# Later stores, states written in place and earlier small weights in a scheduled hybrid decoder layer

## The chip, the core and the metric

The kernel runs on one core of a Trainium2 chip. The metric is the device time of one execution in microseconds (us); the number given is the median of the runs. The engines in the profile are PE (TensorE, matrix products; PEld are its weight loads), DVE (VectorE), ACT (ScalarE), POOL (GpSimd) and SP (SyncE, whose queue issues the transfers).

## The reference

One layer of a hybrid decoder, for a prompt of 2048 tokens and for 8 samples of 8 new tokens (2112 tokens in all), width 1024. Cut to what matters:

```python
xn = rms_norm(x, norm_pre)
z = xn @ w_in                      # 1024 x 4096: v_pool, g_pool, u_lru, g_lru, 1024 columns each
# pool: mean over the last 2, 4, 8 or 16 tokens (4 groups of 256 columns) less the token; a
# 256 x 256 map by group; a scale. A sample's first means reach into its 15 state rows
y_pool = pool_map(window_mean(v_pool) - v_pool) * pool_scale
# lru: causal convolution of width 4, then gates from 128 x 128 blocks and a linear recurrence
xs = conv4(u_lru)
r, i = sigmoid(xs @ wa + ba), sigmoid(xs @ wx + bx)
a = exp(-8 * r * softplus(-lam))
h[t] = a[t] * h[t - 1] + xs[t] * i[t] * sqrt(1 - a[t] ** 2)
mixed = concat(y_pool * silu(g_pool), h * silu(g_lru))
out = x + rms_norm(mixed @ w_out, norm_post)
```

Outputs are the rows for prompt and samples and the new states (the last 15 pool rows, 3 convolution rows, last h).

## The kernel before

**Products.** Everything is float32. Each operand is split in a high part (a cast by ScalarE) and a low part (a subtraction, by VectorE or GpSimd, L310), and each product is three: high·high, high·low, low·high. `hi_lo` (L825) is this split for half tiles of the input weights.

**Tokens and quads.** The tokens lie along the columns, in three macro-tiles m = 0, 1, 2 of 704 columns (the last holds 640 prompt tokens and the 64 sample tokens). The 4096 columns of w_in are 16 quads for each macro-tile: four groups p of the kinds V (pool in), G (pool gate), U (lru in) and L (lru gate). m = 0 uses plain products, with raw weights from w_in split on the way. m = 1 and 2 use a seven-product (Winograd) form of each quad: `a1V`, `e2G` and so on are its partial results. It needs seven sums of quarters of the normalised tokens (X11, T1, T2, X22, X21, T3, T4) and seven of the weights. The weight sums are made and split while m = 0 runs, stored to DRAM (`wsd`), and loaded six products ahead by `w_step` (L870). For the late quads (all of U and L of m = 1, and V and G of its first group) the sums are made in m = 1 itself. The half tiles of weights form a ring of seven.

**The chains around the products.** The partial results are copied or added (L980, L976) into tiles: `e` for V, `u` for U, `g` for the gates. From `e`, `pool_chain` (L1043) makes window sums, `dh` and `dl`, and `pool_map` (L1107) the map with the weights `pw`, into `g`, stored to `mixed` (L1129). From `u`, `conv_chain` (L1134) makes `xs` (L1157, VectorE), its high part `xh` (L1162, ScalarE) and its low part `xl` (L1164, GpSimd); `gate_mm` (L1169) multiplies them by the weights `lw` to the gates `r` and `i`; `lru_chain` (L1192) runs the recurrence, and GpSimd multiplies by the gate and SP stores it to `mixed` (L1233 to L1243). The tiles `t` (16 in all) and `e` (6) are pools: a quad begins when enough are free. The small weights `pw` and `lw` are loaded for m = 0 by `load_small` (L897: L907, L910), split (L915) and stored for the later macro-tiles (L920). For m = 2, `quad_begin` (L930) puts the samples' 15 state rows into `e`: SP loads them into a tile `sp`, of which there is one buffer (L944), and GpSimd copies them into place (L945).

**Between macro-tiles**, `x_chain` (L1251) normalises the next tokens into XA, and `transition` (L1304) makes the seven sums from XA and splits them into XN as their products come up: T2 and T4 in two spare tiles (`t2_tiles`, once `dg` and `rt`), the others in XA.

**The out-projection**, from about 843 us on, is again seven products per block of tokens (p1 to p7); `a` tiles come back from `mixed` (L426), weights from w_out or from combinations of it in DRAM, `wtd` (made and stored in L1365 to L1380, loaded in L378 and split in L1392).

**The order.** A planner in the kernel file writes the order of every engine. The products stand in a fixed row of slots (L1411). The chains are generators that ask for engine time, and a job is granted to the engine that can start it earliest by the planner's own clocks. "t" moves a job's ready time, "D" lets it issue a transfer once that time lies within the present slot. Every engine and the SP queue execute in program order, so an instruction that waits holds back all behind it. For a transfer this reads:

```python
elif e == "t":
    job["ready"] += arg
elif e == "D" and job["ready"] <= end:
    pass
```

Transfers all go through the one SP queue.

Of the kernel before, what the change touches and what calls it, by code (L numbers as in the profile page):

```python
# [10 lines left out]
F32 = mybir.dt.float32  # L11
# [48 lines left out]
TABLE_COST = 1.3  # L60
X_LEAD = (6, 5)
# [6 lines left out]
def hymba_kernel(  # L68
# [827 lines left out]

    def load_small(m, kind, p):  # L897
# [7 lines left out]
        r = t_tile(f"{kind}r{p}")[:, :512]  # L905
        if kind == "pw":
            nc.sync.dma_start(out=r, in_=pool_w[p])  # L907
        else:
            for j in range(2):
                nc.sync.dma_start(out=r[:, 256 * j:256 * (j + 1)], in_=lru_w[2 * p + j])  # L910

        def work():
            yield "t", 4.0
            yield "A", 0.62
            AC.copy(out=t[:, 0, :], in_=r)  # L915
            yield "V", 0.75
            tsub(t[:, 1, :], r, t[:, 0, :].bitcast(F32))
            t_done(1)
            yield "D", 0
# [10 lines left out]
    def quad_begin(q):  # L930
# [3 lines left out]
        for j, blk in enumerate(blocks(kind, p)):  # L934
            if kind == "V":
# [6 lines left out]
                if m == LM:  # L942
                    sp = sb.tile([P, N_S, PB], F32, tag="sp", bufs=1, name=f"sp{blk}")
                    nc.sync.dma_start(out=sp, in_=st_pool[blk])  # L944
                    G.tensor_copy(out=seq8(E, PB + PW, SP_ST, 0, PB), in_=sp)  # L945
# [10 lines left out]
            else:  # L956
                dst.append(t_tile(f"g{blk}_{m}"))

# [84 lines left out]
    def pool_chain(q):  # L1043
# [3 lines left out]
        c = L * 0.00125 + 0.08  # L1047
        ds = []
        for j, blk in enumerate(blocks("V", p)):
# [19 lines left out]
            yield "V", 1.05  # L1069
# [17 lines left out]
        if not m:  # L1087
# [19 lines left out]
    def pool_map(q, j, c):  # L1107
# [12 lines left out]
        def evac():  # L1120
            V.scalar_tensor_tensor(out=g[:, cs], in0=Y, scalar=col(C_SCALE, blk), in1=g[:, cs],  # L1121
                                   op0=ALU.mult, op1=ALU.mult)
            if c == 1:
# [3 lines left out]
                def store():  # L1127
                    yield "D", 0
# [5 lines left out]
    def conv_chain(q, j):  # L1134
# [4 lines left out]
        yield "?", lambda: (not prev or prev.get("gates")) and t_free() >= (3 if j or m else 4)  # L1139
# [15 lines left out]
        for k in range(CB):  # L1155
            yield "V", 1.2
# [6 lines left out]
        yield "G", 1.95  # L1163
        tsub(xl, xs, xh.bitcast(F32), G)  # L1164
# [27 lines left out]
    def lru_chain(q, j, r, gi, v):  # L1192
# [4 lines left out]
        yield "V", 0.95  # L1197
# [6 lines left out]
        yield "V", 0.95  # L1204
        u = t_chain(f"w{m}_{b}")[:, :n]
        V.scalar_tensor_tensor(out=u, in0=r, scalar=1.0, in1=v, op0=ALU.add, op1=ALU.mult)
        yield "V", 0.95
# [4 lines left out]
        yield "V", 0.95  # L1212
# [3 lines left out]
        yield "V", 1.1  # L1216
# [3 lines left out]
        yield "V", 1.8  # L1220
# [8 lines left out]
        yield "G", 2.2  # L1229
        sg = Q[lq]["dst"][j]  # L1230
        if m < LM:
            G.tensor_copy(out=hh[:, b:b + 1], in_=r[:, MW - 1:MW])
            G.tensor_tensor(out=sg[:, :MW], in0=sg[:, :MW], in1=r, op=ALU.mult)  # L1233
        else:
# [3 lines left out]
            G.tensor_tensor(out=sg[:, :PW], in0=sg[:, :PW], in1=r[:, :PW], op=ALU.mult)  # L1238
            G.tensor_tensor(out=as8(sg[:, PW:MW]), in0=as8(sg[:, PW:MW]), in1=seq8(r, PW, SC_ST, CB, S_S),
                            op=ALU.mult)  # L1240
        t_done(1)
        yield "D", 0
# [8 lines left out]
    def x_chain(m):  # L1251
# [34 lines left out]
        for k in range(KT):  # L1286
            yield "V", 0.95
            a = stage_x(k // HK)[:, k % HK, :]
            V.scalar_tensor_tensor(out=a, in0=a, scalar=col(C_NP, k), in1=rt[:, :MW], op0=ALU.mult, op1=ALU.mult)
        t2_tiles[:] = [dg, rt]  # L1290
# [3 lines left out]
    t2_tiles = []  # L1294
# [9 lines left out]
    def transition(m):  # L1304
# [4 lines left out]
        src = {"X11": X(0, 0), "T1": X(0, 0), "T2": t2_tiles, "X22": X(1, 1), "T3": X(0, 1), "X21": X(1, 0),  # L1309
               "T4": t2_tiles}  # L1310
        done = set()

        def put(n, eng="V"):
# [6 lines left out]
            if n == "T4":  # L1320
                t_done(2)

        def chain():
# [36 lines left out]
    def combos_chain():  # L1360
# [9 lines left out]
        for k in range(KT):  # L1370
            yield "D", 0
            r, nxt = nxt, load(k + 1) if k + 1 < KT else None
            for j, o, a, b in ((T1, (0, 0), (0, 1), (0, 0)), (T3, (0, 1), (1, 1), (0, 1)),
# [4 lines left out]
                def store(j=j, k=k, o=r[o]):  # L1378
                    yield "D", 0
# [4 lines left out]
    def region_chain(r, j, k0, k1):  # L1384
# [3 lines left out]
        for k in range(k0, k1):  # L1388
# [4 lines left out]
            yield "V", 0.75  # L1393
# [484 lines left out]
```

## Time and profile before

| what | before |
|---|---|
| median of 3 runs (lowest to highest) | 1195.79 us (1193.86 to 1197.48) |
| the profiled execution | 1194.03 us, span 1192.3 us |
| mean granted clock of PE | 0.98 |
| PE busy, and idle in the span | 1132.6 us, 59.7 us |
| DVE, ACT, POOL busy | 902.9, 653.8, 253.3 us |
| transfers | 322.10 MB, mean 270 GB/s |

Rows of the profile name an instruction as line, engine, operation, written tile, read tiles. In square brackets, or after the last bar of a group, stands how long the engine was idle before it and what released it. The clock column is the mean clock granted to PE in that stretch, as a share of full speed. The view of waits lists per engine the waiting operation, what released it, the total, how often, and the longest. SPq rows are transfers being issued.

### The profile page before, as it was taken

The page shows a single profiled execution, that of the slowest core. Times are in us where ns is not written, and L with a number is a line of the kernel's source. Part 1 is how long each engine was busy: PE and PEld are TensorE (multiplying, and loading weights), DVE is VectorE, ACT ScalarE, POOL GpSimd, SP SyncE. Part 2 cuts the span into 40 slices and gives each one's busy share as a digit, 9 for nine tenths or more (in the row PEclk, how much of TensorE's full clock was granted, in tenths as well). Part 3 has the DMA queues.
Part 4 walks back from the last instruction along what each step waited for, and adds up shares of the span by engine and source line. Part 5 has one row for each costly group of instructions (what it writes and reads, how often), then busy time and mean ns, then how long its engine had stood idle before and what let it go on. Part 6 is the DMA issues. An engine that isn't in the chain of part 4 may idle for free. (4 is left out here: it accounts for less than half of the span.)

```text
span 1192.3 us, 17811 instructions
## 1 busy us (share of the span) xinstructions
PE 1132.6 (95%) x6274; PEld 1055.3 (89%) x6274; DVE 902.9 (76%) x1356; ACT 653.8 (55%) x1109; POOL 253.3 (21%) x284
## 2 busy tenths in 40 slices
PE   7999998988999999999799989999989999999996
PEld 6999998988899999988799979999868888888885
DVE  6779783897978858677688958767586668778777
ACT  5455747758665748666557736455844233344222
POOL 4201100200523030200443512214020003211232
PEclk9999998998999999999899989999989999999998
DMA  9278696936799898998699989999669776776553
GB/s 336 116 269 328 223 330 235 356 139 235 276 315 318 291 333 309 385 360 294 221 334 371 351 340 393 342 333 324 186 169 277 206 212 197 210 233 199 159 177 123
DMA packets 173368, 322.10 MB, mean 270 GB/s; under 512 B 17568, under 2 KB 79264, under 8 KB 173280
## 3 DMA queue, kind: packets, MB, share of 16 engines
q1 hardware_dynamic: 173280, 320.97, 77.9%
q8 instruction: 49, 0.80, 0.3%
q14 instruction: 39, 0.32, 0.1%
HBM read 218.51 MB, written 102.15 MB: 269 GB/s over the span
## 5 line engine op out<-in xcount | busy, mean ns | idle before, releaser
L438 POOL TENSOR_TENSOR xr<-ac,xr 128x512 f32<-128x512 f32 x27 | 46.6, 1745 | 225.8 <-DVE ac L578 120.1
L1157 DVE SCALAR_TENSOR_TENSOR xs<-u,parT,xs 128x704 f32<-128x704 f32 (+1 forms) x72 | 85.3, 1193 | 12.0 <-ACT xs L1146 11.6
L445 PE MATMUL p<-XN,s 128*128 128x512 f32 (+1 forms) x224 | 87.7, 392 | 3.9 <-ACT s L132 3.9
L446 PE MATMUL p<-XN,s 128*128 128x512 f32 (+1 forms) x224 | 87.5, 391 | 0.0
L447 PE MATMUL p<-XN,s 128*128 128x512 f32 (+1 forms) x224 | 87.3, 390 | 0.0
L310 POOL TENSOR_TENSOR xl<-xs,xh 128x704 fp32r<-128x704 f32 (+1 forms) x24 | 45.9, 1910 | 144.1 <-ACT xh L1162 93.9
L241 PE MATMUL zL<-XN,wL 128*128 128x352 f32 x384 | 64.5, 328 | 0.7 <-DVE wL L310 0.7
L241 PEld LDWEIGHTS zL<-XN,wL 128*128 128x128 f32 x384 | 63.2, 192 | 1.3 <-DVE wL L310 1.3
L558 ACT ACTIVATE p<-ac 128x512 f32<-128x512 f32 (+1 forms) x32 | 18.8, 587 | 74.2 <-DVE ac L438 74.2
L241 PE MATMUL y<-dh,pw 128*128 128x352 f32 x192 | 55.2, 329 | 4.4 <-ACT pw L915 2.4
L132 ACT CAST s<-a 128x512 fp32r<-128x512 f32 x48 | 28.8, 616 | 52.8 <-DVE a L438 39.2
L445 PEld LDWEIGHTS p<-XN,s 128*128 128x128 f32 x224 | 42.6, 190 | 14.1 <-ACT s L132 4.4
L438 DVE TENSOR_TENSOR a<-a,a 128x512 f32<-128x512 f32 x48 | 32.9, 690 | 28.5 <-DMA a<-mixed 24.7
L445 PE MATMUL p<-XN,a 128*128 128x512 f32 x137 | 54.0, 394 | 0.0
L447 PE MATMUL p<-XN,a 128*128 128x512 f32 x137 | 54.0, 394 | 0.0
L446 PE MATMUL p<-XN,a 128*128 128x512 f32 x137 | 54.0, 394 | 0.0
L1121 DVE SCALAR_TENSOR_TENSOR g<-y,parT,g 128x352 f32<-128x352 f32 x48 | 27.9, 580 | 31.1 <-PE y L241 31.0
L446 PEld LDWEIGHTS p<-XN,s 128*128 128x128 f32 x224 | 42.6, 190 | 9.8
L447 PEld LDWEIGHTS p<-XN,s 128*128 128x128 f32 x224 | 42.4, 189 | 10.0 <-DVE s L135 0.2
L241 PE MATMUL zU<-XN,wU 128*128 128x352 f32 x288 | 50.3, 329 | 0.0
L241 PE MATMUL zV<-XN,wV 128*128 128x352 f32 x288 | 48.1, 323 | 0.3 <-ACT wV L827 0.2
L241 PEld LDWEIGHTS zU<-XN,wU 128*128 128x128 f32 x288 | 48.1, 194 | 0.0
(352 smaller groups left out, 3293.3 us busy)
## 6 DMA issues: line engine op xcount, KB each, us to landing
a<-mixed SPq DMA_DIRECT2D x112, 256.0 KB, 4.0
mixed<-g SPq DMA_DIRECT2D x48, 352.0 KB, 5.6
w2V<-wsd SPq DMA_DIRECT2D x28, 512.0 KB, 6.9
w2G<-wsd SPq DMA_DIRECT2D x28, 512.0 KB, 5.6
w2U<-wsd SPq DMA_DIRECT2D x28, 512.0 KB, 6.7
w2L<-wsd SPq DMA_DIRECT2D x28, 512.0 KB, 6.8
wsd<-XN SPq DMA_DIRECT2D x27, 512.0 KB, 4.6
w1V<-wsd SPq DMA_DIRECT2D x24, 512.0 KB, 5.3
```

The costliest lines, as they stand in the source:

```text
L132: hi_eng.copy(out=hi, in_=src)
L241: nc.tensor.matmul(out, lhsT=lhsT, rhs=rhs, start=start, stop=stop)
L310: (eng or V).tensor_tensor(out=out, in0=a, in1=b, op=ALU.subtract)
L438: (eng or nc.vector).tensor_tensor(out=out, in0=a, in1=b, op=op)
L445: nc.tensor.matmul(out, lhsT=ah, rhs=wh, start=start and k == 0, stop=False)
L446: nc.tensor.matmul(out, lhsT=ah, rhs=wl, start=False, stop=False)
L447: nc.tensor.matmul(out, lhsT=al, rhs=wh, start=False, stop=stop and k == KT - 1)
L558: nc.scalar.activation(out=junk, in_=o, func=AF.Square, accum_out=st[:, g:g + 1])
L1121: V.scalar_tensor_tensor(out=g[:, cs], in0=Y, scalar=col(C_SCALE, blk), in1=g[:, cs], op0=ALU.mult, op1=ALU.mult)
L1157: V.scalar_tensor_tensor(out=xs, in0=E[:, k:k + n], scalar=col(C_CW + 8 * k, b), in1=xs, op0=ALU.mult, op1=ALU.add)
```

## The change

Five things are done. (1) Stores are given to the queue some time after their data are ready: 4.0 us for weight sums and small weights, 2.0 for `mixed` and `wtd`. The "t" before "D" puts them later in the program's order. (2) The pool states are loaded straight into `e`, as 128 x 8 x 15 numbers with gaps between the rows; the tile `sp` and its copy are gone. (3) The small weights of groups 1 to 3 in m = 0 are loaded when the quad V or U begins, and not when their chain comes to them; this holds one more `t` tile meanwhile, and the conditions on free tiles are raised by one. A delay of 4.0 in front of their split is gone. (4) T2 and T4 are made in place, in the quarter X(0,0) of XA that T1 was made in: T2 as X22 less T1, once T1 is split. The low parts of X22 and X21 are on VectorE, their jobs start with the transition, and the two spare tiles are freed earlier. (5) The low part `xl` is on VectorE. Besides, the planner's durations are changed, and its clock of VectorE is moved on by 0.6 at each long GpSimd job. The core of the diff:

```diff
+LAG = 4.0
+MLAG = 2.0
+XL_ON = "V"
+SG_ON = "G"
...
     def grant(job, start):
         e, dur = job["req"][:2]
+        if e == "G" and dur > 1.5:
+            clock["V"] = max(clock["V"], T[0]) + 0.6
...
     def hi_lo(hi, lo, src, store=None):
...
-        yield "V", 0.75
+        yield "V", 0.71
         tsub(lo, src, hi.bitcast(F32))
         if store:
+            yield "t", LAG
             yield "D", 0
             nc.sync.dma_start(out=w_key(*store[1:]), in_=store[0].bitcast(F32))
...
+    def small_early(kind, p):
+        r = small_raw[kind, p] = t_tile(f"{kind}r{p}")[:, :512]
+        if kind == "pw":
+            nc.sync.dma_start(out=r, in_=pool_w[p])
+        else:
+            for j in range(2):
+                nc.sync.dma_start(out=r[:, 256 * j:256 * (j + 1)], in_=lru_w[2 * p + j])
...
         def work():
-            yield "t", 4.0
             yield "A", 0.62
             AC.copy(out=t[:, 0, :], in_=r)
...
             t_done(1)
+            yield "t", LAG
             yield "D", 0
...
                 if m == LM:
-                    sp = sb.tile([P, N_S, PB], F32, tag="sp", bufs=1, name=f"sp{blk}")
-                    nc.sync.dma_start(out=sp, in_=st_pool[blk])
-                    G.tensor_copy(out=seq8(E, PB + PW, SP_ST, 0, PB), in_=sp)
+                    nc.sync.dma_start(out=seq8(E, PB + PW, SP_ST, 0, PB), in_=st_pool[blk])
...
+        if m == 0 and p and kind in "VU":
+            small_early({"V": "pw", "U": "lw"}[kind], p)
...
                 def store():
+                    yield "t", MLAG
                     yield "D", 0
                     nc.sync.dma_start(out=mixed[:, blk, m * MW:(m + 1) * MW], in_=g[:, :MW])
...
         AC.copy(out=xh, in_=xs)
-        yield "G", 1.95
-        tsub(xl, xs, xh.bitcast(F32), G)
+        yield XL_ON, 0.9 if XL_ON == "V" else 1.95
+        tsub(xl, xs, xh.bitcast(F32), {"V": V, "G": G}[XL_ON])
...
         t_done(1)
+        yield "t", MLAG
         yield "D", 0
         nc.sync.dma_start(out=mixed[:, 8 + b, m * MW:(m + 1) * MW], in_=sg[:, :MW])
...
-        src = {"X11": X(0, 0), "T1": X(0, 0), "T2": t2_tiles, "X22": X(1, 1), "T3": X(0, 1), "X21": X(1, 0),
-               "T4": t2_tiles}
+        src = {"X11": X(0, 0), "T1": X(0, 0), "T2": X(0, 0), "X22": X(1, 1), "T3": X(0, 1), "X21": X(1, 0),
+               "T4": X(0, 0)}
...
+            yield "?", lambda: "T1" in done
             yield "V", 1.75
-            x_raw(t2_tiles, X(1, 1), X(0, 0))
+            x_raw(src["T2"], X(1, 1), src["T1"])
             x_jobs["T2"] = spawn(put("T2"), clock["V"] + HOP, rank=0)
-            x_jobs["X22"] = spawn(put("X22", "G"), T[0], rank=0)
...
             yield "?", lambda: "T2" in done
             yield "V", 1.75
-            x_raw(t2_tiles, X(1, 0), t2_tiles)
-            x_jobs["X21"] = spawn(put("X21", "G"), T[0], rank=0)
+            x_raw(src["T4"], X(1, 0), src["T2"])
...
+        for n in ("X22", "X21"):
+            x_jobs[n] = spawn(put(n), rank=0)
...
                 def store(j=j, k=k, o=r[o]):
+                    yield "t", 2.0
                     yield "D", 0
                     nc.sync.dma_start(out=wtd[:, j, k, :], in_=o)
...
-                while t_free() < {"V": 0}.get(q[2], 2) or (q[2] == "V" and (e_free() < 2 or not sums_done(*q[:2]))):
+                while t_free() < {"V": 0, "U": 2}.get(q[2], 2) + (m == 0 and q[2] in "VU") or (q[2] == "V" and (e_free() < 2 or not sums_done(*q[:2]))):
...
             for k in range(5, KT):
                 src = w_load("b11", k)
                 w_split(0, k, src)
+            clock["A"] += 4.4
+            clock["V"] += 5.0
```

Where the instructions stand now, at three places that the prediction speaks of (line numbers differ between the two files).

The SP queue before, near the end of the first macro-tile; `lwr` are the raw lru weights of the last group, `wr1U` raw weights of m = 1:

```order
L874 DMA w1G_1_3161<-wsd 128x1024
L832 DMA wsd<-w1V_7_3137 128x1024
L874 DMA w1V_4_3201<-wsd 128x1024
L910 DMA lwr_3206<-in_lru_w 128x256 x2
L832 DMA wsd<-w1G_5_3181 128x1024
L339 DMA wr1U_11_3256<-in_w_in 128x512
```

And now; `wr0L` are the raw weights of the last quad of m = 0:

```order
L839 DMA wsd<-wL_22_2557 128x1024
L839 DMA wsd<-wU_11_2656 128x1024
L912 DMA lwr_2730<-in_lru_w 128x256 x2
L343 DMA wr0L_11_2733<-in_w_in 128x512
L343 DMA wr0L_12_2735<-in_w_in 128x512
L343 DMA wr0L_21_2737<-in_w_in 128x512
```

The load of the last group's lru weights has moved from among the weights of m = 1 to ahead of the raw weights of the last quad of m = 0.

The SP queue before, at the start of the out-projection; `w` are weights for its products, `a` tiles of `mixed`, `g_2` the last gates of m = 2:

```order
L378 DMA w_3_8667<-wtd 128x512
L378 DMA w_4_8696<-wtd 128x512
L426 DMA a_0_0_8721<-mixed 128x4x128
L426 DMA a_0_0_8723<-mixed 128x4x128
L426 DMA a_0_1_8725<-mixed 128x4x128
L426 DMA a_0_1_8727<-mixed 128x4x128
L378 DMA w_5_8752<-wtd 128x512
L1243 DMA mixed<-g_2_8348 128x704
L378 DMA w_6_8780<-wtd 128x512
L378 DMA w_7_8791<-wtd 128x512
```

And now, up to the same two weights:

```order
L382 DMA w_4_8637<-wtd 128x512
L382 DMA w_5_8666<-wtd 128x512
L1771 DMA gp<-in_norm_post 128x1024
L1144 DMA mixed<-g_2_8178 128x704
L430 DMA a_0_0_8694<-mixed 128x4x128
L430 DMA a_0_0_8696<-mixed 128x4x128
L430 DMA a_0_1_8698<-mixed 128x4x128
L430 DMA a_0_1_8700<-mixed 128x4x128
L382 DMA w_6_8730<-wtd 128x512
L382 DMA w_7_8746<-wtd 128x512
```

The store of the lru gate is no longer between w_5 and w_6; it comes fourteen rows after w_7.

GpSimd before, where m = 1 passes into m = 2; `e_2` are the first two V tiles of m = 2, the last row the low parts of X22 and X21:

```order
L953 COPY u_1_5475<-hu 128x3
L941 COPY e_2_5768<-hp 128x15
L945 COPY e_2_5768<-sp_5770 128x8x15
L941 COPY e_2_5773<-hp 128x15
L945 COPY e_2_5773<-sp_5775 128x8x15
L310 TENSOR_TENSOR XN<-XA,XN 128x1408 x2
```

VectorE now, at the same place; XA rows are raw sums in place, XN rows low parts:

```order
L314 TENSOR_TENSOR XN<-XA,XN 128x1408
L990 TENSOR_TENSOR g_1_5555<-a1L_5556,g_1_5555 128x352
L314 TENSOR_TENSOR XN<-XA,XN 128x1408
L314 TENSOR_TENSOR dl_31_5707<-s_1_8_5552,dh_31_5671 128x704
L314 TENSOR_TENSOR XN<-XA,XN 128x1408
L314 TENSOR_TENSOR XA<-XA 128x2x352 x2
L1221 SCALAR_TENSOR_TENSOR w_4_5761<-rg_4_5355,xs_1_5044 128x704
L314 TENSOR_TENSOR XN<-XA,XN 128x1408
L1135 SCALAR_TENSOR_TENSOR g_1_5078<-y_5749,parT,g_1_5078 128x352
L314 TENSOR_TENSOR XA<-XA 128x2x352 x2
```

All seven low parts of this transition now stand in VectorE's row, four of them within these ten rows, and no copy of states stands on GpSimd ahead of them.

More of the change, by code (lines that the diff above doesn't have):

```diff
@@ L904, in load_small @@
             return
[L905 to L910, printed above, removed]
+        if (kind, p) not in small_raw:
+            small_early(kind, p)
+        r = small_raw.pop((kind, p))
         def work():
-            yield "t", 4.0
             yield "A", 0.62
             AC.copy(out=t[:, 0, :], in_=r)
-            yield "V", 0.75
+            yield "V", 0.71
             tsub(t[:, 1, :], r, t[:, 0, :].bitcast(F32))
             t_done(1)
+            yield "t", LAG
             yield "D", 0
@@ L1086, in pool_chain @@
         yield "?", lambda: not prev or prev.get("maps")
-        if not m:
+        if not m and not p:
             yield "?", lambda: t_free() >= 1
@@ L1138, in conv_chain @@
         prev = Q.get((m, p - 1, "U") if p else (m - 1, NG - 1, "U"))
-        yield "?", lambda: (not prev or prev.get("gates")) and t_free() >= (3 if j or m else 4)
+        yield "?", lambda: (not prev or prev.get("gates")) and t_free() >= (3 if j or m or p else 4)
         t_live[0] += 3
@@ L1232, in lru_chain @@
             G.tensor_copy(out=hh[:, b:b + 1], in_=r[:, MW - 1:MW])
-            G.tensor_tensor(out=sg[:, :MW], in0=sg[:, :MW], in1=r, op=ALU.mult)
+            SGE.tensor_tensor(out=sg[:, :MW], in0=sg[:, :MW], in1=r, op=ALU.mult)
         else:
@@ L1739, in p1_chain @@
                             prep_11(g + 2)
+                            clock["A"] += 1.3
+                            clock["V"] += 1.4
                         if g + 4 < 5:
```

35 lines of the change are left out of this document (17 added, 18 removed).

## The prediction

> **What bounds the kernel now.** I read the page's busy times first:
>
> ```profile
> PE 1132.6 (95%) x6274; PEld 1055.3 (89%) x6274; DVE 902.9 (76%) x1356; ACT 653.8 (55%) x1109; POOL 253.3 (21%) x284
> ```
>
> TensorE (PE) is busy for 95% of a span of 1192.3 us, and the change leaves its products alone. So the change can only win time in which TensorE stands still, and time in which it runs slowly. The view of waits of that engine names both the waiting operation and what came last for it (columns: total us, times, longest):
>
> ```profile
> PE a2V L239 <- DMA w2V<-wsd: 6.7, 2, 5.8
> ...
> PE e2V L239 <- POOL XN L310: 5.0, 1, 5.0
> PE r L241 <- ACT xh L1162: 4.4, 1, 4.4
> PE p L445 <- ACT s L132: 3.9, 1, 3.9
> PE y L241 <- ACT pw L915: 2.4, 1, 2.4
> PE a1U L239 <- DVE u L976: 2.2, 1, 2.2
> PE a2L L239 <- DMA w2L<-wsd: 1.7, 1, 1.7
> ...
> PE r L241 <- ACT lw L915: 1.5, 1, 1.5
> PE y L241 <- DVE pw L310: 1.5, 1, 1.5
> ...
> PE r L241 <- POOL u L951: 1.4, 1, 1.4
> PE p L241 <- ACT a L132: 1.3, 1, 1.3
> PE e2V L239 <- DVE XN L310: 1.2, 1, 1.2
> ...
> PE r L241 <- DVE lw L310: 0.9, 1, 0.9
> ...
> PE r L241 <- POOL xl L310: 0.8, 1, 0.8
> ```
>
> Few waits, nearly all single, each at its own place. (The 1.4 named after `u` is, by the operation it stands in front of, a product with `xl`.) Then I cut an 8 us stretch from the end of each larger wait, and looked at the granted clock:
>
> ```profile
> 185.50:193.50 8.00, 6.52 (x24) 6.06 (x25) 4.46 (x7) 8.00 (x16) 1.86 (x5) 0.57 0.62 222
> 270.27:278.27 8.00, 6.62 (x23) 6.38 (x24) 5.27 (x7) 6.10 (x10) 1.75 (x3) 0.57 0.91 327
> 324.79:332.79 8.00, 7.07 (x25) 6.78 (x26) 7.27 (x12) 5.99 (x9) 0.00 (x0) 0.57 1.00 352
> 584.62:592.62 8.00, 7.98 (x37) 7.69 (x38) 2.61 (x5) 2.20 (x3) 3.22 (x2) 0.76 0.77 263
> 706.89:714.89 8.00, 8.00 (x37) 8.00 (x38) 4.10 (x7) 0.45 (x1) 0.00 (x0) 0.72 1.03 415
> 879.27:887.27 8.00, 8.00 (x22) 6.27 (x23) 6.92 (x12) 3.23 (x7) 1.87 (x3) 0.61 0.75 205
> ```
>
> Columns are the stretch, its length, busy us of PE, its weight loads, VectorE (DVE), ScalarE (ACT) and GpSimd (POOL), the clock, DMA share and GB/s. After six waits the clock is 0.57 to 0.76, where a stretch without them has 1.00 (below). A wait therefore costs itself and, behind it, (1 − clock) × the busy time of PE: 2.8, 2.8, 3.0, 1.9, 2.2 and 3.1 us in the order of the rows.
>
> After the wait of 2.2 for `u` there is no such loss:
>
> ```profile
> 555.50:563.50 8.00, 7.98 (x49) 7.80 (x50) 4.13 (x6) 5.49 (x8) 0.00 (x0) 1.00 0.91 321
> ```
>
> **Part by part.** All in the profiled run's time, 1194.03 us. It lies 1.8 below the median of the runs before, so 1.8 is added at the end.
>
> *Small weights a quad or more earlier.* The first part of this (A) is the pool map at 185, the second (C) the lru gates at 324:
>
> ```profile
> 176.65 0.44 SPq L907 DMA_DIRECT2D pwr<-in_pool_w  x1
> ```
>
> ```profile
> 184.83 0.62 ACT L915 CAST pw<-pwr 128x512 fp32r<-128x512 f32 x1 [10.46 <-DMA pwr<-in_pool_w]
> ```
>
> ```profile
> 324.12 0.62 ACT L915 CAST lw<-lwr 128x512 fp32r<-128x512 f32 x1 [0.91 <-DMA lwr<-in_lru_w]
> ```
>
> The load goes out 8.2 us ahead of the cast; ScalarE waits 10.46 for it, the cast comes, VectorE makes the low part, and TensorE waits for both. Issued a quad earlier, the data is there, and the cast of 0.62 and the subtraction can run ahead of need. A: 2.4 + 1.5 + clock 2.8 = 6.7. C: 1.5 + 0.9 + 3.0 = 5.4. The cost is one `t` tile more held for a quad, bounded below by nothing and above by one new wait; it goes into the allowance below.
>
> *Pool states straight into their place.* The two loads of a pair share one buffer, so the second stands in the queue until the first has landed and GpSimd has copied it. Behind it stand weights:
>
> ```profile
> 695.49 6.86 SPq L944 DMA_DIRECT2D sp<-in_st_pool  x2
> 702.44 0.38 SPq L874 DMA_DIRECT2D w2V<-wsd  x1
> ```
>
> TensorE's 5.8 at 706 (E) waits for that w2V. With the buffer gone, two issues remain, and the queue is free about 6 us earlier, more than the wait: 5.8 + 2.2 = 8.0. A later pair blocks the queue in the same way, and 0.9 (the rest of 6.7) and 1.7 are waited for w2V and w2L after it: 2.6, which go too. What is next to be late is whatever the loads themselves need to land; the same two stalls' tiles are issued six products ahead when nothing blocks. The states now come in 1024 pieces of 60 bytes per block rather than 128 of 480. No transfer of this kind is in the trace; the nearest rows are these (KB each, then median us to landing):
>
> ```profile
> as<-mixed SPq DMA_DIRECT2D x4, 128.0 KB, 2.8
> ...
> sp<-in_st_pool SPq DMA_DIRECT2D x8, 60.0 KB, 3.2
> ```
>
> `as` has 512 pieces of 256 bytes in 2.8, so 1024 pieces take between 2.8 and 5.6. Only the first window sum of VectorE needs them, over ten us later; I take 5.6, and nothing on the path. The Trainium skill ("DMA: Bandwidth & Descriptors", Specifications) puts the smallest transfer at full rate at 512 bytes, with a read-modify-write below it. It speaks against the smaller pieces; by it the loads would be slower still, but both rows above lie below 512 bytes already, and no run so far shows 60.
>
> *Stores later in the queue.* At 879 (F) TensorE waits 3.9 for `s`, and the chain is in three rows, two of the queue and one of ScalarE:
>
> ```profile
> 872.57 0.33 SPq L1243 DMA_DIRECT2D mixed<-g  x1
> 873.00 0.88 SPq L378 DMA_DIRECT2D w<-wtd  x2
> ```
>
> ```profile
> 876.29 0.62 ACT L1392 CAST XN<-w 128x512 fp32r<-128x512 f32 x1 [4.65 <-DMA w<-wtd]
> ```
>
> The store waits for its data and holds back two weight loads; ScalarE waits for these, and its next cast is `s`. In the new order these two loads stand ahead of that store: 3.9 + 3.1 = 7.0. Behind the store then stand loads of a later product, which have slack.
>
> *X combinations in place, X22 and X21 on VectorE.* At 584 (D) TensorE waits 5.0 for GpSimd:
>
> ```profile
> 573.49 5.82 POOL L945 COPY e<-sp 128x120 f32<-128x120 f32 x1 [35.22 <-DMA sp<-in_st_pool]
> ...
> 581.40 6.31 POOL L310 TENSOR_TENSOR XN<-XA,XN 128x1408 fp32r<-128x1408 f32 x2
> ```
>
> The copies that delay GpSimd are gone, and so is its subtraction: 5.0 and 1.2 (for XN of VectorE, 573) and 1.9 = 8.1. But T2 now is made from T1's tile, after T1's own split, with one subtraction and one cast behind one another; I leave 2.0 of waiting there. D: 6.1.
>
> *xl on VectorE.* TensorE's waits for it, 0.8 and 1.4, go: 2.2. Price on VectorE from the groups of operations (us in all, then mean ns):
>
> ```profile
> L310 POOL TENSOR_TENSOR xl<-xs,xh 128x704 fp32r<-128x704 f32 (+1 forms) x24 | 45.9, 1910 | 144.1 <-ACT xh L1162 93.9
> ```
>
> ```profile
> L310 DVE TENSOR_TENSOR dl<-s,dh 128x704 fp32r<-128x704 f32 x24 | 23.1, 962 | 14.9 <-ACT dh L1093 14.6 <-issue 0.3
> ```
>
> 24 × 0.962 for xl, and 4 × 2 × 0.962 for X22 and X21, which have twice the elements: 30.8 us of new VectorE work. It is hidden wherever VectorE has time: of the seven stretches above one has it busy for over 7 of 8 us. Bounds are 0 and 30.8; I take a fifth, 6.2.
>
> *The stall B at 270* (4.4 for xh, behind casts that wait for raw weights) loses its blockers only in part; of 4.4 + 2.8 I count half, 3.6. At 843, 1.3 goes: the casts of the last weights stand ahead of others now.
>
> *What the new order brings.* Every quad's instructions are re-ordered, `t` tiles are held longer by the late stores and by the early weights, and at the end of the first macro-tile three slots of U and L have nothing but maps and gates between them. Something new will be late. The six clock stalls cost 6.7 + 5.4 + 8.0 + 7.0 + 8.1 + 8.6 = 43.8, 7.3 each; I allow two of them, 14.6, between none and six.
>
> Sum: 6.7 + 5.4 + 8.0 + 2.6 + 7.0 + 6.1 + 2.2 + 3.6 + 1.3 = 42.9, less 6.2 and 14.6, leaves 22.1. 1194.0 − 22.1 + 1.8 = **1173.7**.
>
> **The rivals.**
>
> *VectorE becomes the limit.* Two thirds of 30.8 on the path instead of a fifth is 14.3 more: 1188.0. For it: VectorE has 7.27 of 8 us in the stretch at 324. Against it: 76% overall, and GpSimd's 45.9 us no longer run beside it.
>
> *Short waits do not draw the slow clock.* 2.2 for `u` is followed by 1.00, while A and C have no wait over 2.4 and yet 0.57. If something other than these waits slowed the clock there, 2.8 + 3.0 stay: 1179.5. The Trainium skill ("TensorE: Matmul & The Clock Gate", Part 1, What's actually happening) puts half clock after at least one idle window of about 3.4 us, free-running; by that rule two gaps of 1.5 and 0.9 could not bring it, and the trace disagrees at 324. Two waits close together seem to count, so a small chance.
>
> *The new order brings as much as it takes.* Six new stalls of 7.3 in place of two: 43.8 against 42.9: about 1196, no change.
>
> *Slower: late stores hold the half tiles.* In the second macro-tile, U and L weights are still being summed, in a ring of seven half tiles, each free when TensorE has read it and its store has landed. From the view of tile w1U (first start) and the transfers:
>
> ```profile
> L239 PE MATMUL a1U<-XN,w1U x192: 318/323/428, 345.2 to 557.4; 128*128 128x352 f32 x192
> ```
>
> ```profile
> L310 DVE TENSOR_TENSOR w1U<-wr1U,w1U x16: 679/685/924, 336.0 to 541.3; 128x512 fp32r<-128x512 f32 x16
> ```
>
> ```profile
> wsd<-w1U SPq DMA_DIRECT2D x16, 512.0 KB, 4.9
> wsd<-w1L SPq DMA_DIRECT2D x16, 512.0 KB, 4.7
> ```
>
> The low part is done at 336.7, the store goes 4.0 later and lands 4.9 after that: 345.6. TensorE reads the tile until 345.2 + 6 × 0.323 = 347.1. So the tile is freed by TensorE with 1.5 us to spare. If stores land later than about 6.4, tiles are held; at 7.9 every one of the 32 is held 1.5 us: 48 on the path, against 42.9 gained: 1194.0 + 1.8 − 42.9 + 48 = 1200.9, slower. Against it: the landing rows.
>
> The change does do what it says, as far as the new order shows.
>
> **How the numbers follow.** A measurement of this kernel can tell about 0.3%, 3.6 us, from no change. The forecast (1152 to 1183 by the allowance from none to 24) has 0.62; the clock rival 0.05; VectorE as limit 0.13: together 0.80 for faster. As many stalls as removed: 0.08, the same. Held tiles: 0.12, slower. The low end is the sum with nothing new: 1194.0 − 42.9 + 1.8 = 1153, less 1 for what B may give besides: 1152. The high end takes in VectorE as limit and 1 us of spread: 1189. Outside lie the last two rivals, 0.20.
>
> **What would show it.** Right: no TensorE wait for pw or lw of ScalarE near 185 and 324, none for w2V over 1 us after a load of states, no GpSimd row with XN of 128x1408 after 300 us, no wait of 3.9 for `s`; fewer stretches under 0.8 of the clock, two or three instead of six; VectorE near 930 us. Wrong: as many half-clock stretches as before at other places, VectorE named for most new waits (then the fifth was too small), casts of w1U or w1L waiting for transfers in the second macro-tile (held tiles), or window sums waiting for `in_st_pool` (60-byte pieces).

## The result, and the profile after

The changed kernel takes 1178.91 us (median of 4 runs, 1177.78 to 1183.18), the kernel before 1194.82 (4 runs). The ratio is 0.9871, with a 95% interval of 0.984 to 0.9903: faster by 1.29%, about 15.4 us. The prediction was 1173.7, 22.1 us below the median of before that it started from (1195.79). So the sign and the range held, and 70% of the forecast gain came.

The profiled run after took 1178.76 us, with a span of 1177.0 and a mean clock of 0.987. Its busy times, from the page:

```profile
PE 1127.4 (96%) x6274; PEld 1053.1 (89%) x6274; DVE 897.8 (76%) x1380; ACT 659.7 (56%) x1108; POOL 187.7 (16%) x248
```

VectorE has 24 instructions more and is busy for less (902.9 before); GpSimd is busy for 66 us less. TensorE's waits, from the view of waits, all of over 1.8 us but the first of the kernel:

```profile
PE a2V L243 <- ACT XN L329: 4.5, 2, 3.7
PE a1G L243 <- DMA w1G<-wsd: 3.7, 1, 3.7
PE zV L245 <- ACT wV L833: 3.7, 1, 3.7
PE e2L L243 <- DMA w2L<-wsd: 2.6, 1, 2.6
PE a2V L243 <- DVE XN L314: 2.5, 2, 1.2
PE a1V L243 <- ACT e L994: 2.2, 1, 2.2
PE a2V L243 <- DMA w2V<-wsd: 2.1, 2, 1.9
PE p L451 <- DVE s L139: 1.9, 1, 1.9
```

The waits for pw, lw, xl and xh, and for GpSimd's XN, are gone. The 3.9 for s at the start of the out-projection is 1.2, and the 5.8 for w2V behind the states is 1.9 (at 690). Most of the list has no counterpart before: its waits stand at eight places, 83, 304, 504, 558, 574, 690, 765 and 1147 us, and none is over 3.7, where the longest before were 5.8 and 5.0. The stretches of 8 us behind six of them (columns as in the prediction; the one at 575 takes 574) show the slow clock again; those of before are in the prediction:

```profile
83.20:91.20 8.00, 7.65 (x37) 7.36 (x38) 7.96 (x12) 6.75 (x12) 0.22 (x2) 0.79 0.93 311
304.55:312.55 8.00, 8.00 (x40) 8.00 (x41) 5.99 (x10) 5.84 (x8) 0.52 (x1) 0.79 0.98 318
504.00:512.00 8.00, 8.00 (x44) 8.00 (x45) 7.23 (x7) 4.21 (x7) 3.48 (x5) 0.81 1.06 380
575.40:583.40 8.00, 8.00 (x40) 8.00 (x41) 3.23 (x4) 4.42 (x7) 0.09 (x1) 0.79 0.26 101
690.02:698.02 8.00, 7.44 (x28) 7.02 (x29) 3.73 (x7) 0.78 (x2) 0.00 (x0) 0.58 0.96 345
765.51:773.51 8.00, 8.00 (x40) 8.00 (x41) 3.57 (x4) 1.97 (x4) 0.00 (x0) 0.79 1.03 417
```

Added up over the whole run after 40 us: TensorE's idle times of 0.2 us and more (timeline) were 40.2 us before and are 28.8 now; the busy time lost to the slow clock ((1 − clock) × busy, in stretches of 2 us) was 15.8 and is 11.1. Together 16.1 less, against a span that is 15.3 shorter. So the whole difference is in these two sums, and the account to settle is 56.0 us before against 39.9 now. In stretches of 1 us, the time at half clock is 6.8 us long in each of the six places of before, and 3.4 us in five of the six of now (6.8 at 690).

### The profile page after: what moved, and what is told of

It reads as the page before. It is cut to its first block, busy times and chain, and to the rows that moved or that the text cites. A ratio compares the mean times of both kernels' runs of the same rounds, so it can differ in the third digit from the quotient of the medians.

```text
span 1177.0 us, 17796 instructions
## 1 busy us (share of the span) xinstructions
PE 1127.4 (96%) x6274; PEld 1053.1 (89%) x6274; DVE 897.8 (76%) x1380; ACT 659.7 (56%) x1108; POOL 187.7 (16%) x248
## 5 line engine op out<-in xcount | busy, mean ns | idle before, releaser
L442 POOL TENSOR_TENSOR xr<-ac,xr 128x512 f32<-128x512 f32 x27 | 50.9, 1904 | 211.6 <-DVE ac L582 107.1
L1172 DVE SCALAR_TENSOR_TENSOR xs<-u,parT,xs 128x704 f32<-128x704 f32 (+1 forms) x72 | 72.0, 1010 | 2.9 <-ACT xs L1161 2.7
L245 PEld LDWEIGHTS zV<-XN,wV 128*128 128x128 f32 x288 | 47.6, 193 | 4.6 <-ACT wV L833 3.9
L245 PE MATMUL zU<-XN,wU 128*128 128x352 f32 x288 | 47.7, 322 | 0.0
L245 PE MATMUL zG<-XN,wG 128*128 128x352 f32 x288 | 47.2, 323 | 0.0
```

Source lines behind the costliest of these rows:

```text
L245: nc.tensor.matmul(out, lhsT=lhsT, rhs=rhs, start=start, stop=stop)
L442: (eng or nc.vector).tensor_tensor(out=out, in0=a, in1=b, op=op)
L1172: V.scalar_tensor_tensor(out=xs, in0=E[:, k:k + n], scalar=col(C_CW + 8 * k, b), in1=xs, op0=ALU.mult, op1=ALU.add)
```

## The experiments

My theory after the result was this: the change repairs six stalls, worth some 40 us, and its new order brings others back. Rivals: the gain comes from one part alone; the order alone, made anew by the planner's numbers, makes the difference; the repairs are worth less, because each wait moves to the next engine. The first kernels undo one part of the changed kernel. The last five add one part, or four, to the kernel before, **with TensorE's and ScalarE's instructions left in the order of before** (but for one row of TensorE): they are written so that the planner, which otherwise makes a new order at each edit, has the same figures to order by. Where nothing else is said, the time is a median of 6 runs, and the ratio goes against runs of before on the same chip.

**Pool states as rows of 480 bytes, in two buffers** (in the changed kernel; only rows of the queue and of GpSimd differ; here and in the later kernels with two buffers, the small tile `s8` of the start is put in one of them to make room):

```diff
-                    nc.sync.dma_start(out=seq8(E, PB + PW, SP_ST, 0, PB), in_=st_pool[blk])
+                    sp = sb.tile([P, N_S, PB], F32, tag="sp", bufs=2, name=f"sp{blk}")
+                    nc.sync.dma_start(out=sp, in_=st_pool[blk])
+                    G.tensor_copy(out=seq8(E, PB + PW, SP_ST, 0, PB), in_=sp)
```

> The changed kernel, but the pool states come as rows of 480 bytes into a small tile, of which there are now two, and GpSimd copies them into place; the order of TensorE, ScalarE and VectorE is the same, instruction by instruction. Theory (issue of the small pieces holds the queue: two loads 3.35 us and the weight load behind them 2.98 us): the waits for w2V and w2G at 690 to 693 (1.9 and 0.6) and for w2L at 765 (2.6) go, with the slow clock behind them: 6 to 10 us faster than the changed kernel, about 1170. Rival (the share of the transfers is full there, the pieces do not matter): within 2 us of the changed kernel, about 1179. Second rival (GpSimd's copy comes late to the first window sum): slower, over 1181.

Measured: 1173.49 us, 0.9857 (0.9833 to 0.9881), about 2 us below the changed kernel by the ratios and 5 by the medians; the intervals overlap. The queue in the changed kernel, then in this one:

```profile
679.18 3.35 SPq L957 DMA_DIRECT2D e<-in_st_pool  x2
682.62 2.98 SPq L881 DMA_DIRECT2D w2V<-wsd  x1
```

```profile
679.61 1.30 SPq L958 DMA_DIRECT2D sp<-in_st_pool  x2
681.01 0.42 SPq L881 DMA_DIRECT2D w2V<-wsd  x1
```

Two loads of small pieces and the one behind them hold the queue for 6.3 us, those of long rows for 1.7. The 1.9 for w2V at 690 is gone and the 2.6 at 765 is 1.3; others of 1.4 for w2G and 1.7 for w2L stand there instead, but none of them draws the slow clock, which lost 4.8 us in this part of the changed kernel. The queue does what the theory says. The gain in time lies between the theory (6 to 10) and the rival (within 2), and its size is not settled. The landing is hardly different, in the changed kernel and here:

```profile
e<-in_st_pool SPq DMA_DIRECT2D x8, 60.0 KB, 6.7
```

```profile
sp<-in_st_pool SPq DMA_DIRECT2D x8, 60.0 KB, 6.3
```

So the price of the pieces, as far as these rows show it, is in the issue and not in the landing.

**Weight stores without their delay** (in the changed kernel; only the queue's rows are moved):

```diff
-LAG = 4.0
+LAG = 0.0
```

> The changed kernel with the stores of weight sums and small weights issued as soon as their data are planned to be ready (4.0 us to 0); the order of the four computing engines is the same, only the queue's differs. Theory (a store that waits for VectorE holds weight loads behind it, so the delay is part of the gain): new waits of TensorE for wsd loads, 3 to 8 us slower, 1182 to 1187. Rival (the queue has slack, or late stores hold half tiles and their removal gives time back): 1177 to 1180, or faster.

Measured: 1178.02 us, 0.989 (0.9868 to 0.9911): the changed kernel's time. The rival holds: beside the other parts, this delay shows no gain in time. The waits of the theory did come, though: those for w2 weights are 9.1 us in all, against 6.7 in the changed kernel. In this profile they are offset by the slow clock, which costs 7.9 us and not 11.1, partly because the same wait of 2.18 at 305 did not draw it here.

**xl on GpSimd again**, at the same places (11 runs):

```diff
-        tsub(xl, xs, xh.bitcast(F32), {"V": V, "G": G}[XL_ON])
+        tsub(xl, xs, xh.bitcast(F32), G)
```

> The changed kernel with xl computed by GpSimd at the same places of the program; the order of the other engines is the same. Theory (GpSimd beside VectorE slows VectorE, and a product waits for xl's 1.9 us): TensorE waits before products with xl come back in some of the 24 places, 2 to 6 us slower, 1181 to 1185, and VectorE's instructions that lie beside GpSimd's are longer again. Rival (the engine of xl is off the path): 1178 to 1180.

Measured: 1182.94 us, 0.9933 (0.9911 to 0.9954): slower than the changed kernel by 0.6% of before's time by the ratios and by 4.0 us by the medians. But products hardly wait for xl (once, 0.3); the wait at 304 grew from 2.2 to 3.7, and that for w2G near 697 from 0.6 to 2.2. The groups of xl, first here, then in the changed kernel:

```profile
L314 POOL TENSOR_TENSOR xl<-xs,xh 128x704 fp32r<-128x704 f32 (+1 forms) x24 | 48.0, 1998 | 197.8 <-ACT xh L1177 156.8 <-issue 40.8
```

```profile
L314 DVE TENSOR_TENSOR xl<-xs,xh 128x704 fp32r<-128x704 f32 (+1 forms) x24 | 21.4, 894 | 7.5 <-ACT xh L1177 7.5
```

VectorE's busy time is nearly the same without this work:

```profile
PE 1129.3 (95%) x6274; PEld 1054.0 (89%) x6274; DVE 898.6 (76%) x1356; ACT 660.0 (56%) x1108; POOL 231.5 (20%) x272
```

In the changed kernel it is 897.8, with 21.4 for xl. So 21.4 us of new work are paid by 22.2 us that VectorE's other instructions save when GpSimd does not make xl beside them. The theory has the direction; the mechanism is its second half, not the waits for xl.

**The delay put back for group 0's small weights** (12 runs):

```diff
         def work():
+            if not p:
+                yield "t", 4.0
             yield "A", 0.62
```

> The changed kernel with the delay of 4.0 us put back ahead of the split of the small weights of group 0, which are not loaded early; the planner orders the rest anew. Theory (without the delay the cast of lw stands at the head of ScalarE's queue 12.2 us before its data land, and the silu and the casts of wV behind it come late): the wait of 3.7 at 83 us and its slow clock of 1.6 go, about 5 us faster, 1174, if the rest of the order is as good. Rival (the raw weights of V land late in any case): the wait stays at over 2 us.

Measured: 1189.95 us, 0.9978 (0.9954 to 1.0002). The wait at 83 is gone, as the theory says; this row of the changed kernel, the first load that is not early, was its cause:

```profile
76.48 0.62 ACT L928 CAST lw<-lwr 128x512 fp32r<-128x512 f32 x1 [12.23 <-DMA lwr<-in_lru_w]
```

ScalarE stood for 12.2 us in front of data that was on its way; silu and the casts of wV stood behind. With the delay back, the same cast comes at 76.24, after 7.2 us of waiting, and two silu and two copies are done ahead of it. But the planner made a new order of the rest, and in it new waits came up, so that almost the whole gain of the change was lost:

```profile
PE a2V L243 <- DMA w2V<-wsd: 6.1, 2, 3.9
...
PE a2V L243 <- ACT XN L329: 5.5, 2, 3.7
PE a1G L243 <- ACT g L996: 3.6, 2, 2.3
```

The condition of my expectation, "if the rest of the order is as good", failed. So the edits that follow leave the order alone, but for the two of the planner's numbers.

**Low parts of X22 and X21 on GpSimd again**, at the same places:

```diff
-            x_lo(n, src[n], {"V": V, "G": G}[eng])
+            x_lo(n, src[n], G if n in ("X22", "X21") else V)
```

> The changed kernel with the low parts of X22 and X21 executed by GpSimd at the same places; the other engines' order is the same. Theory (GpSimd takes 3.3 us where VectorE takes 1.6, but VectorE has other work): in the passage from m = 1 to 2 TensorE waits up to 1.7 us more at each of two places, and 2.2 at 304 becomes under 1, since VectorE is free for wr1V there: 0 to 4 us slower. Rival (VectorE's load at the passages is what gives the gain back): 3 to 6 us faster.

Measured: 1182.49 us, 0.9927 (0.99 to 0.9954). Slower than the changed kernel by 0.6% of before's time by the ratios (the intervals just overlap) and by 3.6 us by the medians. That is near the theory's size, but not its way: the wait at 304 is 3.8 and not shorter. VectorE's load does not give the gain back; the rival falls. (In the passage from m = 1 to m = 2 TensorE waits 1.5 for VectorE's XN where it waited 0.8, the rest as in the changed kernel.)

**The changed kernel with the planner's old numbers** (durations and clock pushes; the work of all five changes stays):

```diff
-        if e == "G" and dur > 1.5:
-            clock["V"] = max(clock["V"], T[0]) + 0.6
...
-            yield "V", 0.97
+            yield "V", 1.2
...
-            clock["A"] += 4.4
-            clock["V"] += 5.0
...
```

> The changed kernel with the planner's durations and clock pushes of before; all five changes of the work stay. It shows how far the order alone, made anew, moves the time. Theory (the changes of the work carry the gain): within 5 us of the changed kernel, 1174 to 1184. Rival (the planner's numbers carry it): over 8 us slower, 1187 or more.

Measured: 1207.22 us, 1.0124 (1.009 to 1.0157): slower than before, 28 us slower than the changed kernel. The theory (within 5 us) is wrong, and the rival's mark of 1187 is passed. The longest of TensorE's waits:

```profile
PE a2G L243 <- DMA w2G<-wsd: 8.7, 3, 4.0
...
PE a2V L243 <- ACT XN L329: 4.5, 2, 3.7
PE a1G L243 <- DVE g L988: 3.1, 1, 3.1
PE p L245 <- ACT a L136: 2.8, 1, 2.8
```

**The kernel before with the new numbers alone** (5 runs; this order changes the rows of the layer's output, so it is read as an order only, and its time is weak evidence):

> The kernel before with nothing but the planner's new durations and clock pushes. Theory (the stalls come from the pool states, the small weights and GpSimd, which numbers do not cure): 1188 to 1200, with the waits for w2V behind the states and for GpSimd's XN still there. Rival (the numbers carry the gain): 1183 or less.

Measured: 1209.81 us, 1.0146 (1.0114 to 1.0179). Neither theory holds: the numbers are worth −28 us in the changed kernel and +18 in the kernel before. So the numbers are no gain in themselves: they help with one set of instructions and hurt with the other. A new order as such moves the time by more than any part of the change does.

**The kernel before with two buffers for the pool states**, every engine's order that of before:

```diff
-                    sp = sb.tile([P, N_S, PB], F32, tag="sp", bufs=1, name=f"sp{blk}")
+                    sp = sb.tile([P, N_S, PB], F32, tag="sp", bufs=2, name=f"sp{blk}")
```

> The kernel before with two buffers for the pool states instead of one; every engine's and the queue's order is that of before, instruction by instruction. Theory (the second load of a pair holds the queue until GpSimd has copied the first): the queue's waits of 6.9 us at the loads of states go, and with them the wait of 5.8 for w2V at 706 with 2.2 of slow clock and most of 2.6 after 772; the copies come earlier too, so part of the 5.0 for GpSimd's XN at 584 may go: 8 to 13 us faster than before, 0.989 to 0.993. Rival (the transfers themselves are late): within 3 us of before.

Measured: 1181.09 us, 0.991 (0.9877 to 0.9943). The pair of loads that took 6.86 in the queue:

```profile
689.62 1.63 SPq L944 DMA_DIRECT2D sp<-in_st_pool  x2
```

The waits at 706 and at 772 to 779 are gone, that for GpSimd's XN is 3.2, with 1.0 behind it, and not 5.0. The gain is 0.9%, 10 us, for one tile of 480 bytes by partition: the theory is shown.

**The kernel before with all stores later**, by the delays of the change:

```diff
+    def put_later(lag, out, in_):
+        def store():
+            yield "t", lag
+            yield "D", 0
+            nc.sync.dma_start(out=out, in_=in_)
+        spawn(store(), rank=3)
...
-            nc.sync.dma_start(out=w_key(*store[1:]), in_=store[0].bitcast(F32))
+            put_later(4.0, w_key(*store[1:]), store[0].bitcast(F32))
...
-        nc.sync.dma_start(out=mixed[:, 8 + b, m * MW:(m + 1) * MW], in_=sg[:, :MW])
+        put_later(2.0, mixed[:, 8 + b, m * MW:(m + 1) * MW], sg[:, :MW])
...
```

> The kernel before with all stores issued later by the change's own delays (4.0 us for weight sums and small weights, 2.0 for mixed and wtd), the order of ScalarE and GpSimd being that of before and that of TensorE and VectorE but for one row or two. In this order the last gate's store comes after w_6, but still ahead of w_7. Theory (the delays by themselves cure little; in the changed kernel the store was moved by the new order): the wait of 3.9 for s near 879 stays at over 2 us, 0 to 3 us faster than before. Rival (the delays carry the gain of that wait, and free the queue at other places): 6 to 9 us faster.

Measured: 1179.73 us, 0.99 (0.9868 to 0.9932). The rival was right. The wait of 3.9 for s is 0.9, though w_7 still stands behind the store. And it cures more: no wait for pw at 185. The cast's row is now

```profile
178.56 0.62 ACT L922 CAST pw<-pwr 128x512 fp32r<-128x512 f32 x1 [5.04 <-DMA pwr<-in_pool_w]
```

The load of pwr is issued at 168.5 and not at 176.7, since the queue waits less for VectorE at stores of XN there (2.8 us between 150 and 180, and 8.1 before) and two of these stores now stand behind the load. The stall A thus had two cures, and either was enough. That fits the changed kernel, which has both and lost no time without the delay of the weight stores.

**The kernel before with xl, X22 and X21 on VectorE**:

```diff
-            x_lo(n, src[n], {"V": V, "G": G}[eng])
+            x_lo(n, src[n], V)
...
-        tsub(xl, xs, xh.bitcast(F32), G)
+        tsub(xl, xs, xh.bitcast(F32), V)
```

> The kernel before with xl and the low parts of X22 and X21 executed by VectorE at the places where the planner had GpSimd; the order of TensorE, ScalarE and the queue is that of before. Theory: the wait of 5.0 for GpSimd's XN at 584 goes or falls under 2, with its slow clock of 1.9, and so do 0.8 and 1.4 before products with xl; the 30.8 us of new work are hidden or offset by VectorE's shorter instructions beside an idle GpSimd: 5 to 9 us faster than before. Rival (VectorE is what waits end on at the passages and in the lru chains): no change, or up to 6 us slower.

Measured: 1182.53 us, 0.9915 (0.9884 to 0.9947). The gain, 9 us by the medians, is at the upper end of the theory's. The wait for XN at 584 is gone but for 1.2, and the two waits for lw at 325 are gone too. Against that, in TensorE's list:

```profile
PE r L241 <- DVE xl L310: 2.0, 2, 1.6
```

VectorE is busy for 900.4 us, where 902.9 + 30.8 was to be feared.

**The kernel before with the small weights early** (11 runs; the tile is taken when quad V or U begins, and the planner's count of tiles is left as it was):

```diff
...
+        if m == 0 and p and kind in "VU":
+            small_early({"V": "pw", "U": "lw"}[kind], p)
```

> The kernel before with the small weights of groups 1 to 3 loaded when quad V or U of m = 0 begins; the order of the four computing engines is that of before, only the queue's rows are moved. Theory: the waits for pw at 185 (2.4 and 1.5) and for lw at 325 (1.5 and 0.9) go with their slow clock of 2.8 and 3.0: 10 to 13 us faster than before. Rival (the cast and the subtraction stand too late in the order of their engines): under 4 us faster, with both waits there.

Measured: 1183.72 us, 0.9933 (0.9911 to 0.9955), 8 us. The wait at 185 is gone. The one for lw is not:

```profile
PE r L241 <- DVE lw L310: 1.8, 1, 1.8
```

It is 0.5 and 1.8 instead of 1.5 and 0.9, and only its slow clock (3.0) is gone. The early load can't be thanked for that: with all stores later the same two waits, 0.5 and 1.8, are followed by a clock of 0.79. The theory is right for pw; for lw the rival is: the subtraction stands late in VectorE's order.

**All four on the order of before**: two buffers, small weights early, VectorE for the low parts, stores later (the lru gates' by 8.0, which puts the last behind w_7; the rest of the edit is as above):

```diff
...
-        nc.sync.dma_start(out=mixed[:, 8 + b, m * MW:(m + 1) * MW], in_=sg[:, :MW])
+        put_later(8.0, mixed[:, 8 + b, m * MW:(m + 1) * MW], sg[:, :MW])
```

> The kernel before with four repairs on its own order: two buffers for the pool states, the small weights early, xl and the low parts of X22 and X21 by VectorE, and the stores later by 4.0 and 2.0 as in the change, but by 8.0 for the gates of the lru group, which puts the last of them behind w_7. TensorE's and ScalarE's order stays that of before. Theory (the change loses in its new order about half of what the repairs give): the waits at 185, 325, 584, 706, 772 to 779 and 879 go and nothing takes their place: 28 to 36 us faster than before, 1155 to 1163. Rival (each repair moves the wait on to the next engine): about the changed kernel's time, 1175 to 1182.

Measured: **1158.16 us** (1155.28 to 1160.16), 0.971 (0.9684 to 0.9737). This beats both kernels: 33.6 us below before, as the theory has it (28 to 36), and some 21 below the changed kernel. The rival, that each repair moves the wait on, falls. Page and waits:

```profile
PE 1118.6 (97%) x6274; PEld 1044.6 (90%) x6274; DVE 897.2 (78%) x1384; ACT 654.5 (57%) x1109; POOL 199.2 (17%) x256
```

```profile
PE z L241 <- ACT w L1461: 5.4, 1, 5.4
PE r L241 <- DVE xl L310: 4.6, 2, 3.6
PE r L241 <- ACT xh L1180: 2.2, 1, 2.2
PE p L447 <- DVE s L135: 1.9, 1, 1.9
PE e2G L239 <- DMA w2G<-wsd: 1.8, 1, 1.8
```

The first is the start of the kernel. After 40 us the idle times are 18.5 us and the loss by the clock 3.3: 21.8, against 56.0 before and 39.9 in the changed kernel. Singly the four parts gave 0.9, 1.0, 0.85 and 0.67%, 3.4% in all; together they give 2.9%. So no part carries the gain alone, and the overlap is small, about the price of A (6.7), which had two cures. Each ratio is uncertain by some 0.3%, though.

## Why the prediction was right, and where its sizes were off

*The six stalls and their slow clock.* This step held in the main. In the changed kernel A, B, C and GpSimd's part of D are gone, and F is down to 1.2. E is not: at 690 stand 1.9 and 0.6, with 3.1 of slow clock, in place of 5.8 and 2.2. On the old order the four repairs give 34 us; there B keeps 2.2 and 1.0, with 1.6 of slow clock. The clock's share was counted rightly as part of a stall's price: it fell by 12.5 of 15.8 us with the four repairs.

*Which edit cures which stall.* Partly wrong. A goes by the store delays alone as by the early load; C (325) does not go by the early load, which I said it would, but by taking GpSimd's work away. F (879) needs a delay of 2.0, not the new order that I quoted for it. On the old order E goes when the single buffer does, as said.

*"Two issues remain, and the queue is free about 6 us earlier."* This is the term that was most mis-sized. I counted 8.0 + 2.6 = 10.6 for it; in the changed kernel nothing of it came. TensorE's waits for w2 weights and the slow clock behind them were 8.9 and 2.2 us before, and are 6.7 and 4.8 now. The step holds for long rows: with two buffers on the old order these waits are 0.4. Issued in pieces of 60 bytes, the pair and the load behind it hold the queue for 6.3 us (the single buffer: 6.86 for the pair alone). I had put the risk on the landing, with 5.6 us; that was 6.7, and no wait for it is seen.

*T2 in place, 2.0.* Mis-sized. In the passage from m = 1 to m = 2 TensorE waits 0.8 and 1.2 at 558, then 3.7 and 1.2 at 574: 6.9, and 1.5 for the clock. The longest is T4's; ScalarE and VectorE in the changed kernel:

```profile
572.33 1.36 ACT L329 CAST XN<-XA 128x1408 fp32r<-128x1408 f32 x1 [6.43 <-DVE XA L314]
```

```profile
570.61 1.68 DVE L314 TENSOR_TENSOR XA<-XA 128x704 f32<-128x704 f32 x2
```

T4's raw sum stands in VectorE's order behind additions of partial results that TensorE has yet to deliver. With T2 and T4 in spare tiles, and all low parts on VectorE (the last experiment), there are two waits of 1.2 there. The wait of 3.7 is not the accident of one order: it stands at 3.7 in the two other orders of the changed kernel too (the delay put back, the old numbers). But no kernel puts only T2 back into spare tiles in the new order, so how much is due to the tile and how much to the place in VectorE's order is not settled.

*VectorE's new work, a fifth of 30.8 on the path.* Wrong in sign for VectorE's busy time: it is 5 us less in the changed kernel, where I named 930 as the sign. The row of xl had 0.89 us and not the 0.96 I took, and the saving beside an idle GpSimd, which I named and left out of the sum, was as large as the cost. Some of the work is on the path even so: on the old order with all four repairs a product waits 3.6 for xl at 494, with 1.7 of slow clock.

*The delay of 4.0 that was removed.* The prediction gave it no price. For groups 1 to 3 the load is early; for group 0 it is not, and ScalarE now stands for 12.2 us before that cast: 3.7 of waiting at 83 and 1.6 of slow clock.

*The allowance, two stalls of 7.3.* Too few and too long. The changed kernel has six stretches of slow clock, as many as before and not the two or three that I named as the sign of being right, at 1.5 to 3.1 each, and waits of 1.9 to 3.7 in front of them. My price of 7.3 came from six stretches of 6.8 us at half clock; five of the new ones last 3.4. Against the repairs on the old order, the new order and the parts that go with it (in place, pieces, no delay) cost 39.9 − 21.8 = 18.1 us; I had allowed 14.6 and 6.2, 20.8. The repairs give 56.0 − 21.8 = 34.2 and not 42.9, since on the old order, too, a wait of 3.6 for xl at 494 and some of 1 to 2 come up. So the gains were put 8.7 too high and the costs 2.7 too high, and that the time came within some 5 us is in part the luck of errors that offset each other.

*The rivals.* VectorE as the limit: not seen, but for the wait for xl above. Held half tiles: the stores of w1U land in 6.6 us (median), just beyond my point of 6.4, and yet the queue waits for them 4 times with 3.4 us in all; with the delay at 0 the time is the same. As many new stalls as removed: so in number, six for six, which I had named as a sign of being wrong; they are shorter, and so the gain is there.

*The clock rival.* Short waits do draw the slow clock, but not always. The same wait of 2.18 us for e, in the same order, is followed by 0.79 in the changed kernel (row above) and by full clock with the states in two buffers:

```profile
305.22:313.22 8.00, 8.00 (x50) 8.00 (x51) 7.10 (x12) 5.99 (x8) 0.52 (x1) 1.00 0.93 301
```

The rule of the Trainium skill ("TensorE: Matmul & The Clock Gate", Part 1, What's actually happening), half clock after at least one idle window of about 3.4 us, disagrees with 0.79 after 2.18 us; that the window runs freely, which it also states, agrees with the two outcomes.

## What to carry to other kernels

A queue that runs in order turns one small resource (a buffer of 480 bytes, a store issued with its data not ready) into a stall of the engine that matters, far away; look for what stands ahead of the late load. When a program's order is made by a planner, test each part with the order held fixed: the planner's new numbers alone moved the time by −28 us on one kernel and +18 on the other, more than any part was worth (8 to 12), and so they can hide or fake a gain. Four repairs on the old order were worth twice the change that came with a new one (which also had the states in small pieces, T2 in place and a delay taken out).

## What the runs showed of the hardware

The slow clock follows waits of very different length. At the start of the out-projection a wait of 1.35 us for `a` was followed by a clock of 0.79 on the old order with all stores later, and the same wait of 1.35 by 1.00 with the small weights early; a wait of 3.2 us for GpSimd's XN was followed by 1.00 with two buffers. In all these traces, apart from the end of the kernel, a slow stretch was at half clock for 3.4 us or a multiple of it. Where it came behind one wait or a close pair, it cost 1.4 to 3.4 us (3.9 behind a row of four). The same wait may or may not draw it, so a stall's price is the wait itself and from 0 to 3.4 us more.

The cost of small pieces in a load was the queue's time to issue it: 3.35 us for two loads of 1024 pieces of 60 bytes each, and 2.98 for the next load, against 1.30 and 0.42 with 128 rows of 480 bytes; the landing differed by 0.4 us.

VectorE's other instructions were shorter when GpSimd did not make xl beside them: with xl on VectorE, 21.4 us of new work in 24 instructions left its busy time where it was (897.8 us, and 898.6 with xl on GpSimd).
